# Top-k search of a sparse-attention layer: two groups of three blocks in place of four groups

## The chip, the cores and the metric

One core of one Trainium2 chip runs the whole layer in one launch. The metric is the device time of one execution in microseconds (us), as the median of several runs. Engines are named TensorE (PE; PEld is its weight load), VectorE (DVE), ScalarE (ACT), GpSimd (POOL) and SyncE (SP, which issues loads).

## What is computed

A hybrid decoder layer over 1024 tokens of width 1024, batch 1: a token mixer of two attention groups, a cross attention to 256 memory tokens, and a convolutional GLU. The part that matters here is group A, attention over the 256 best keys by a separate index score, per query and causal:

```python
logits = jnp.einsum('bqhd,bsd->bqhs', qib, k_idx)
score = jnp.einsum('bqh,bqhs->bqs', wib, jax.nn.relu(logits)).astype(jnp.float32)
score = jnp.where(causal[None], score, -jnp.inf)
_, idx = lax.top_k(score, topk)
...
s = jnp.where(valid[:, :, None, :], s, -jnp.inf)
p = jax.nn.softmax(s, axis=-1).astype(v.dtype)
return jnp.einsum('bqhk,bqkd->bqhd', p, v_sel)
```

Group B is differential attention over all causal keys: (softmax(q1 k1) - lam softmax(q2 k2)) v, with 4 heads.

## The kernel before, in words

The 1024 queries are eight blocks of 128; block i sees (i + 1) * 128 keys. Blocks 0 and 1 have at most 256 keys and need no search. For blocks 2 to 7 the kernel finds the 256th largest score of each row, turns it into an additive mask `mb[i]`, and computes group A densely with that mask.

The program runs in stages. **C**: the input projection in five column chunks (`proj_mm`, 24 matmuls a tile, evacuated by ScalarE at L618), with the index scores `sc[i]` made on the way (`idx_head`, L489 to L496). **B**: 32 units of group B, head by head and block by block in the order 7, 1, 6, 0, 5, 3, 4, 2 (`b_s`: scores, their evacuation with row minimum on VectorE at L746, the exponential on ScalarE at L748; `b_comb`: L756 to L758 on VectorE; `b_t`: transposes, copied by ScalarE at L654; `b_av`), mixed with the key and value projections of the memory (`mem_step`). **A**: 64 units of group A, block by block (`a_s`: scores, evacuated with the mask on VectorE at L991, the exponential at L992; then transposes and `a_av`), with the output projection behind it. Then cross attention and the GLU.

The search is a binary search on the bits of the threshold, 32 rounds from bit 31 to bit 0 (`topk_iter`). One round of a group handles all its blocks:

- On ScalarE ("act"): for each block a Sign of score minus candidate that adds up along the row (L525). VectorE then decides for each block whether the bit stays (L527), and makes the next candidate for the whole group (L529). The next round's Signs wait for it.
- On VectorE ("dve"): for each block a comparison that counts (L537), then two short instructions for the group, which have as many columns as it has blocks: L539 and L540 for the upper 16 bits, L542 and L543 for the lower 16. The upper half compares a 16-bit copy of the scores. After bit 16 the scores are narrowed into another 16-bit copy (L552 and L553, a pair for each 512 columns).

After bit 0 an end step for each block (`topk_mask`, L566 to L579) makes the mask: a count, two comparisons, a scan (L577) that settles ties in order of the keys, and two more passes.

The rounds wait in two queues, `topk_q["act"]` and `topk_q["dve"]`, group after group. A group's rounds may start when its last block's scores are there. `tick(us)` is called after each projection tile, each unit of B and A and each memory unit with the time that this piece is meant to take; where a queue's owed time reaches its `PACE` of the stage (C, B, A), the next round is issued at that place. `topk_finish(i)`, ahead of block i's scores in A, issues whatever of its group is left. The final order on each engine is set by the framework's scheduler, and each engine works through its list in order.

Of the kernel before, what the change touches and what calls it, by code (L numbers as in the profile page):

```python
# [44 lines left out]
def hybrid_layer(ctx, tc, I, out):  # L45
    nc = tc.nc
    pe, act, dve, pool, sp = nc.tensor, nc.scalar, nc.vector, nc.gpsimd, nc.sync
# [20 lines left out]
    def mtile(shape, dt, name):  # L68
        return along.tile(shape, dt, name=name)
# [429 lines left out]

    GROUPS = [(x.split("-")[0], tuple(int(y) for y in x.split("-")[1])) for x in 'act-23,act-6,dve-45,dve-7'.split(",")]
    cand = [mtile([P, 3], I32, f"cand{g}") for g in range(len(GROUPS))]
    ccnt = [mtile([P, 3], F32, f"ccnt{g}") for g in range(len(GROUPS))]
    crej = [mtile([P, 3], I32, f"crej{g}") for g in range(len(GROUPS))]
    cx = [mtile([P, 3], F32, f"cx{g}") for g in range(len(GROUPS))]
    U16 = mybir.dt.uint16
# [5 lines left out]
    def topk_iter(g, b):  # L513

        on, blocks = GROUPS[g]
        ng = len(blocks)
# [42 lines left out]
    def topk_mask(g, j):  # L559

        on, blocks = GROUPS[g]
        i = blocks[j]
# [24 lines left out]
    last = {}  # L587
    scored = [1]

    PACE = [dict(zip(("act", "dve"), [float(y) for y in x.split(",")])) for x in '4,6:4.5,10:4.5,5'.split(':')]  # L590
    phase = [0]

    def tick(us):

        pace = PACE[phase[0]]
        for on in ("act", "dve"):
# [1084 lines left out]
```

## Time and profile before

| | |
|---|---|
| median of 3 runs | 1703.17 us (1700.48 to 1704.67) |
| profiled execution | 1704.6 us, its span 1702.5 us |
| mean granted TensorE clock | 0.968 |
| TensorE busy | 1580.2 us, 93% of the span |
| VectorE busy | 1224.4 us, 72% |
| ScalarE busy | 788.5 us, 46% |
| GpSimd busy | 639.6 us, 38% |

The busy shares are averages over stages with different limits, so the rows further down are cut by stage: busy time of each engine in a stretch, what an engine waited for and who released it, and the mean duration of each kind of instruction. In the names, a number behind a buffer is left out; "jk<-mb,cx 128x768" writes jk and reads mb and cx, 128 partitions by 768 columns.

### The profile page before, as it was taken

What the parts mean: (1) busy time and instruction counts of PE and PEld (TensorE: products, weight loads), DVE (VectorE), ACT (ScalarE), POOL (GpSimd) and SP (SyncE); (2) the same over time, 40 slices, a digit from 0 to 9 for tenths busy, and PEclk for the clock granted to TensorE, in tenths of its full rate; (3) what the DMA queues carried; (4) which work ended last, traced back from release to release, by engine and by line L of the source; (5) the groups of instructions that cost most, each with busy time, mean ns of one, the idle gap of its engine ahead of it and who ended that gap; (6) DMA issues with size and microseconds to landing.
All of it is one profiled execution on the core that took longest, in us unless ns stands there. A gap on an engine that the chain in (4) does not pass through costs nothing.

```text
span 1702.5 us, 22404 instructions
## 1 busy us (share of the span) xinstructions
PE 1580.2 (93%) x7660; PEld 1294.8 (76%) x7660; DVE 1224.4 (72%) x2501; ACT 788.5 (46%) x1633; POOL 639.6 (38%) x787
## 2 busy tenths in 40 slices
PE   8899988778889999999999979999999999988889
PEld 7788766666678888878777857888888888876767
DVE  5746998998988674367552699766666667689974
ACT  6544677587777446325441235333333333433242
POOL 2646666534573352230010145222232221339831
PEclk9999999888989999999999989999999999998999
DMA  8321124212221222261211211222222225842221
GB/s 284 92 82 61 66 93 164 70 49 86 82 81 63 69 74 74 75 211 50 75 43 69 75 74 62 75 88 95 77 74 75 74 77 179 325 147 94 80 75 50
DMA packets 91745, 162.37 MB, mean 95 GB/s; under 512 B 14960, under 2 KB 34928, under 8 KB 91632
## 3 DMA queue, kind: packets, MB, share of 16 engines
q1 hardware_dynamic: 84736, 136.83, 24.7%
q10 hardware_dynamic: 5616, 19.93, 3.0%
q0 software_dynamic: 1280, 4.20, 0.6%
q8 instruction: 60, 0.98, 0.2%
q14 instruction: 53, 0.43, 0.1%
HBM read 126.32 MB, written 34.60 MB: 95 GB/s over the span
## 4 chain that ended last, share of the span: by engine, by line
PE 57%; DVE 27%; issue 7%; DMA 4%; ACT 3%; POOL 2%; SPq 0%; ACTq 0%; DVEq 0%; POOLq 0%
PE acc L281 9%; PE acc L282 9%; PE acc L283 9%; DVE wp L1547 5%; PE big L281 4%; PE big L282 4%; PE big L283 4%; PE trp L281 3%; DVE jk L537 3%; PE trp L282 3%; PE trp L283 3%; PE acc L1009 2%; DVE e L746 2%; PE big L1242 2%; DVE e L758 1%
## 5 line engine op out<-in xcount | busy, mean ns | idle before, releaser
L175 ACT CAST wp<-raw 128x512 fp32r<-128x512 f32 (+1 forms) x204 | 121.2, 615 | 228.5 <-POOL raw L201 127.8
L178 DVE TENSOR_TENSOR wp<-raw,wp 128x512 fp32r<-128x512 f32 (+1 forms) x168 | 134.9, 808 | 117.1 <-ACT wp L175 109.4
L178 POOL TENSOR_TENSOR wp<-raw,wp 128x512 fp32r<-128x512 f32 x84 | 113.5, 1369 | 47.3 <-ACT wp L175 46.5
L199 POOL TENSOR_TENSOR ws<-raw 128x512 f32<-128x512 f32 x21 | 28.4, 1353 | 271.9 <-DMA raw<-in_w_ffn_in_dram 216.4
L281 PE MATMUL acc<-wp,xh 128*128 128x512 f32 (+1 forms) x272 | 110.3, 407 | 9.6 <-ACT X L618 9.6
L282 PE MATMUL acc<-wp,xh 128*128 128x512 f32 (+1 forms) x272 | 110.1, 406 | 0.0
L283 PE MATMUL acc<-wp,xl 128*128 128x512 f32 (+1 forms) x272 | 109.9, 405 | 0.0
L177 POOL TENSOR_SCALAR wp<-raw 128x512 fp32r<-128x512 f32 (+1 forms) x48 | 33.7, 706 | 163.7 <-DVE rst L110 63.5
L654 ACT COPY pt<-trp 128x512 f32<-128x512 f32 (+3 forms) x144 | 66.1, 476 | 61.4 <-PE trp L663 61.1
L525 ACT ACTIVATE mb<-sc,cand 128x384 bf16<-128x384 f32 (+1 forms) x96 | 75.5, 787 | 38.6 <-DVE cand L529 34.5
L1009 PEld LDWEIGHTS acc<-va_t,pt 128*128 128x128 f32 x576 | 74.9, 195 | 9.8 <-ACT pt L654 7.9
L1009 PE MATMUL acc<-va_t,pt 128*128 128x65 f32 x576 | 77.0, 273 | 4.6 <-ACT pt L654 4.5
L991 DVE CUSTOM_DVE_ANT_0 ea<-big,mb,ra 128x384 f32<-128x384 f32 (+5 forms) x48 | 45.5, 948 | 36.9 <-PE trp L663 30.6
L281 PEld LDWEIGHTS acc<-wp,xh 128*128 128x128 f32 x272 | 52.9, 195 | 23.3 <-ACT X L618 11.8
L282 PE MATMUL acc<-wp,wp 128*128 128x512 f32 x152 | 62.3, 410 | 6.5 <-DVE wp L1547 3.8
L282 PE MATMUL big<-wp,wp 128*128 128x512 f32 x132 | 55.0, 416 | 12.4 <-DVE wp L1547 12.3
L281 PE MATMUL acc<-wp,wp 128*128 128x512 f32 x152 | 61.9, 407 | 3.8 <-ACT wp L1546 2.8
L992 ACT ACTIVATE ea<-ea,sta 128x128 f32<-128x128 f32 (+7 forms) x64 | 49.5, 777 | 27.5 <-DVE sta L991 26.4
L1547 DVE TENSOR_TENSOR wp<-ta,wp 128x512 fp32r<-128x512 f32 x55 | 50.7, 962 | 15.5 <-ACT wp L1546 15.5
L283 PEld LDWEIGHTS acc<-wp,xl 128*128 128x128 f32 x272 | 52.8, 194 | 11.5
L282 PEld LDWEIGHTS acc<-wp,xh 128*128 128x128 f32 x272 | 52.6, 194 | 11.3 <-issue 0.2
L283 PE MATMUL acc<-wp,wp 128*128 128x512 f32 x152 | 60.5, 398 | 0.0
(431 smaller groups left out, 5220.2 us busy)
## 6 DMA issues: line engine op xcount, KB each, us to landing
raw<-in_w_ffn_in_dram SPq DMA_DIRECT2D x44, 512.0 KB, 3.7
u_d<-fg ACTq DMA_DIRECT2D x22, 512.0 KB, 3.2
raw<-u_d SPq DMA_DIRECT2D x33, 256.0 KB, 3.1
raw<-in_w_in_dram SPq DMA_DIRECT2D x16, 512.0 KB, 3.9
raw<-in_w_out_dram SPq DMA_DIRECT2D x16, 512.0 KB, 3.6
xraw<-in_x_dram SPq DMA_DIRECT2D x8, 512.0 KB, 7.5
qk_d<-X SPq DMA_DIRECT2D x16, 256.0 KB, 2.0
raw<-in_w_xk_dram SPq DMA_DIRECT2D x8, 512.0 KB, 3.8
```

The source lines that it names most:

```text
L175: act.copy(pg[:, 0, :n], src)
L178: (dve if el == "d" else pool).tensor_tensor(pg[:, 1, :n], src, pg[:, 0, :n].bitcast(F32), op=OP.subtract)
L281: pe.matmul(o, lhsT=lh, rhs=rh, start=start, stop=False)
L282: pe.matmul(o, lhsT=lh, rhs=rl, start=False, stop=False)
L283: pe.matmul(o, lhsT=ll, rhs=rh, start=False, stop=stop)
L525: act.activation(mb[i], sc[i], AF.Sign, bias=cf[:, j:j + 1], scale=-1.0, accum_out=cnt[:, j:j + 1])
L537: dve.tensor_scalar(jk[:, :n], src, th[:, j:j + 1], None, op0=OP.is_ge, op1=OP.add, accum_out=cnt[:, j:j + 1])
L654: act.copy(dst, src)
L991: last["dve"] = dve.tensor_tensor_reduce(e[:, :n], S[:, :n], mask, ra[:, i, h:h + 1], 3.0e38, OP.add, OP.min, st[:, 0, h:h + 1])
L992: last["act"] = act.activation(e[:, :n], e[:, :n], AF.Exp, bias=st[:, 0, h:h + 1], scale=-1.0)
L1009: pe.matmul(acc[:, hh * 65:hh * 65 + 65], lhsT=pt, rhs=va_t[:, kt, :], start=kt == 0, stop=kt == i)
L1547: dve.tensor_tensor(pg[:, 1, :], v, pg[:, 0, :].bitcast(F32), op=OP.subtract)
```

## The change

Two lines. The four groups, (2, 3) and then (6) on ScalarE, (4, 5) and then (7) on VectorE, become two, (2, 3, 6) and (4, 5, 7). The pace, the time between rounds on each engine in C, B and A, is set anew.

```diff
@@ -499,7 +499,7 @@
-    GROUPS = [(x.split("-")[0], tuple(int(y) for y in x.split("-")[1])) for x in 'act-23,act-6,dve-45,dve-7'.split(",")]
+    GROUPS = [(x.split("-")[0], tuple(int(y) for y in x.split("-")[1])) for x in 'act-236,dve-457'.split(",")]
@@ -587,7 +587,7 @@
-    PACE = [dict(zip(("act", "dve"), [float(y) for y in x.split(",")])) for x in '4,6:4.5,10:4.5,5'.split(':')]
+    PACE = [dict(zip(("act", "dve"), [float(y) for y in x.split(",")])) for x in '5.5,8:8,10:4,5'.split(':')]
```

Group (2, 3, 6) can start when block 6's scores are there and group (4, 5, 7) when block 7's are; the first had to wait for block 3, the second for block 5.

How instructions stand on an engine before and after shows at three places. First ScalarE in C, from one projection tile's squares (L629, t2) to the next tile's evacuation (L618, X); mb is the Signs' output by block. Before:

```order
L629 ACTIVATE t2_285_2013<-X_282_1999 128x512
L525 ACTIVATE mb2_930,ccnt0_523<-sc2_931,cand0_519 128x384
L525 ACTIVATE mb3_932,ccnt0_523<-sc3_933,cand0_519 128x512
L525 ACTIVATE mb2_930,ccnt0_523<-sc2_931,cand0_519 128x384
L525 ACTIVATE mb3_932,ccnt0_523<-sc3_933,cand0_519 128x512
L618 ACTIVATE X_288_2051<-acc_287_2026,rx_72 128x512
```

and with the change:

```order
L629 ACTIVATE t2_277_1944<-X_273_1926 128x512
L525 ACTIVATE mb2_922,ccnt0_521<-sc2_923,cand0_519 128x384
L525 ACTIVATE mb3_924,ccnt0_521<-sc3_925,cand0_519 128x512
L525 ACTIVATE mb6_930,ccnt0_521<-sc6_931,cand0_519 128x896
L618 ACTIVATE X_280_1982<-acc_279_1957,rx_72 128x512
```

Two rounds of two Signs ahead of the evacuation have become one round of three; another such round stands ahead of the squares.

Second VectorE at the end of B, ahead of the first score evacuation of A (L991). Before, the last round of block 6 (two more such rounds stand between it and the last unit's L758) and the first instructions of its end step:

```order
L527 TENSOR_SCALAR crej1_528<-ccnt1_524 128x1
L529 SCALAR_TENSOR_TENSOR cand1_520<-crej1_528,cand1_520 128x1
L566 TENSOR_SCALAR mb6_938<-sc6_939,cand1_520 128x896
L569 ISA jk_896_4785,tks_535<-mb6_938,sc6_939 128x896
L569 ISA tks_535 128x1
L571 TENSOR_SCALAR jk_897_4787,ccnt1_524<-sc6_939,tks_535 128x896
L574 TENSOR_SCALAR mb6_938<-sc6_939,tks_535 128x896
L991 ISA ea_928_4926,sta_926_4922<-big_927_4923,tri_68,ra_75 128x128
```

and with the change, ahead of that L991, a round of blocks 4, 5 and 7 and the first count of the next (one more round stands between these rows and the last unit's L758):

```order
L537 TENSOR_SCALAR jk_933_4829,ccnt1_522<-mb4_926,cx1_526 128x640
L537 TENSOR_SCALAR jk_934_4831,ccnt1_522<-mb5_928,cx1_526 128x768
L537 TENSOR_SCALAR jk_935_4833,ccnt1_522<-mb7_932,cx1_526 128x1024
L542 TENSOR_SCALAR crej1_524<-ccnt1_522 128x3
L543 SCALAR_TENSOR_TENSOR cx1_526<-cx1_526,crej1_524 128x3
L537 TENSOR_SCALAR jk_942_4879,ccnt1_522<-mb4_926,cx1_526 128x640
L991 ISA ea_954_4920,sta_952_4916<-big_953_4917,tri_68,ra_75 128x128
```

Three short rounds and the start of an end step became seven counts and two decisions; what is left of the last round and the end steps of blocks 4, 5 and 7 stand behind this L991.

Third VectorE in A, at the first units of block 2. Before, a round of block 7 among the evacuations:

```order
L991 ISA ea_1048_5328,sta_1046_5324<-big_1047_5325,mb2_930,ra_75 128x384
L991 ISA sta_1046_5324 128x1
L537 TENSOR_SCALAR jk_1049_5333,ccnt3_526<-mb7_940,cand3_522 128x1024
L991 ISA ea_1053_5345,sta_1046_5324<-big_1052_5342,mb2_930,ra_75 128x384
L991 ISA sta_1046_5324 128x1
L539 TENSOR_SCALAR crej3_530<-ccnt3_526 128x1
L991 ISA ea_1057_5361,sta_1046_5324<-big_1056_5358,mb2_930,ra_75 128x384
L991 ISA sta_1046_5324 128x1
L540 SCALAR_TENSOR_TENSOR cand3_522<-crej3_530,cand3_522 128x1
```

and with the change, where the end step of block 7 is just finishing (L578 and L579):

```order
L991 ISA ea_1079_5342,sta_1073_5325<-big_1078_5339,mb2_922,ra_75 128x384
L991 ISA sta_1073_5325 128x1
L578 SCALAR_TENSOR_TENSOR jk_1011_5123<-sc7_933,tks_527,jk_1011_5123 128x1024
L991 ISA ea_1083_5358,sta_1073_5325<-big_1082_5355,mb2_922,ra_75 128x384
L991 ISA sta_1073_5325 128x1
L579 TENSOR_TENSOR mb7_932<-mb7_932,jk_1011_5123 128x1024
L991 ISA ea_1094_5388,sta_1073_5325<-big_1093_5385,mb2_922,ra_75 128x384
L991 ISA sta_1073_5325 128x1
```

Behind it the evacuations stand without any search between them.

## Rows read from the trace of the kernel before

**Rows 1.** Stretches C, B, A01, A2-7: length; busy PE, PEld, DVE, ACT, POOL; clock; DMA; GB/s

```profile
143.67:291.60 147.93, 131.55 (x543) 102.11 (x542) 133.99 (x350) 96.90 (x222) 97.34 (x156) 0.95 0.31 101
291.60:481.70 190.10, 152.79 (x888) 130.25 (x888) 173.71 (x475) 142.45 (x343) 88.79 (x143) 0.90 0.23 71
481.70:510.50 28.80, 23.49 (x133) 20.19 (x132) 26.27 (x77) 17.86 (x48) 22.62 (x37) 0.82 0.32 101
510.50:683.00 172.50, 165.78 (x1143) 147.78 (x1142) 113.73 (x249) 94.62 (x166) 62.93 (x113) 0.99 0.21 70
```

**Rows 2.** Waits of VectorE in B: engine, line, released by; us in total, times, longest

```profile
DVE crej L527 <- ACT mb L525: 5.9, 5, 1.7
DVE st L756 <- ACT e L748: 5.1, 5, 1.6
```

**Rows 3.** Waits of TensorE in C

```profile
PE acc L281 <- ACT X L618: 9.6, 5, 3.9
```

**Rows 4.** Waits of ScalarE in C

```profile
ACT mb L525 <- DVE cand L529: 26.5, 19, 3.2
```

**Rows 5.** Counts of VectorE, groups by line and form: busy us, mean ns

```profile
L537 DVE TENSOR_SCALAR_CACHE_REDUCE jk<-mb,cx 128x1024 bf16<-128x1024 uint16 x16 | 20.4, 1275 | 0.1
L537 DVE TENSOR_SCALAR_CACHE_REDUCE jk<-mb,cx 128x768 bf16<-128x768 uint16 x16 | 16.1, 1005 | 0.1
L537 DVE TENSOR_SCALAR_CACHE_REDUCE jk<-mb,cx 128x640 bf16<-128x640 uint16 x16 | 13.9, 871 | 0.0
L537 DVE TENSOR_SCALAR_CACHE_REDUCE jk<-sc,cand 128x1024 bf16<-128x1024 f32 x1 | 1.3, 1270 | 0.0
```

**Rows 6.** Decisions of VectorE, groups by line and form

```profile
L527 DVE TENSOR_SCALAR crej<-ccnt 128x1 int32<-128x1 f32 x96 | 13.1, 145 | 7.8 <-ACT mb L525 7.7
L529 DVE SCALAR_TENSOR_TENSOR cand<-crej,cand 128x1 int32<-128x1 int32 x32 | 8.1, 255 | 0.3
L542 DVE TENSOR_SCALAR crej<-ccnt 128x2 f32<-128x2 f32 x16 | 4.9, 305 | 0.0
L543 DVE SCALAR_TENSOR_TENSOR cx<-cx,crej 128x2 f32<-128x2 f32 x16 | 6.5, 404 | 0.1
L539 DVE TENSOR_SCALAR crej<-ccnt 128x2 int32<-128x2 f32 x16 | 4.7, 291 | 0.0
L540 DVE SCALAR_TENSOR_TENSOR cand<-crej,cand 128x2 int32<-128x2 int32 x16 | 7.8, 490 | 0.1
L542 DVE TENSOR_SCALAR crej<-ccnt 128x1 f32<-128x1 f32 x16 | 2.4, 151 | 0.4
L543 DVE SCALAR_TENSOR_TENSOR cx<-cx,crej 128x1 f32<-128x1 f32 x16 | 5.5, 345 | 0.4
```

**Rows 7.** Narrowing and end steps, groups by line over the span

```profile
L552 DVE TENSOR_SCALAR tk<-sc,cand,crej 128x512 f32<-128x512 f32 (+2 forms) x6 | 2.7, 489 | 0.1
L553 DVE TENSOR_TENSOR mb<-tk,cand 128x512 uint16<-128x512 uint16 (+2 forms) x6 | 3.3, 582 | 0.0
L571 DVE TENSOR_SCALAR_CACHE_REDUCE jk<-sc,cand 128x640 bf16<-128x640 f32 (+2 forms) x3 | 3.2, 1051 | 0.0
L574 DVE TENSOR_SCALAR mb<-sc,cand 128x640 bf16<-128x640 f32 (+2 forms) x3 | 3.0, 1016 | 0.0
L576 DVE TENSOR_SCALAR jk<-sc,cand 128x640 bf16<-128x640 f32 (+2 forms) x3 | 2.5, 842 | 0.0
L577 DVE TENSOR_TENSOR_SCAN sc<-jk 128x384 f32<-128x384 bf16 (+5 forms) x6 | 10.6, 1772 | 0.0
L578 DVE SCALAR_TENSOR_TENSOR jk<-sc,tks,jk 128x384 bf16<-128x384 f32 (+5 forms) x6 | 7.6, 1258 | 0.0
L579 DVE TENSOR_TENSOR mb<-mb,jk 128x384 bf16<-128x384 bf16 (+5 forms) x6 | 3.5, 577 | 0.1
```

**Rows 8.** Signs of ScalarE: the page's group, then block 6's form

```profile
L525 ACT ACTIVATE mb<-sc,cand 128x384 bf16<-128x384 f32 (+1 forms) x96 | 75.5, 787 | 38.6 <-DVE cand L529 34.5
L525 ACT ACTIVATE mb<-sc,cand 128x896 bf16<-128x896 f32 x32 | 33.3, 1041 | 11.3 <-DVE cand L529 8.0 <-DVE st L756 3.3
```

## Prediction

> **What bounds the kernel now.** First the stretches around the search: the rows of busy time per engine over four of them [rows 1]. I cut at fixed VectorE instructions, so that the same cuts can be found in the changed order: C, from the first head sum L631 to the first combination L758; B, from there to the first score evacuation L991 of group A; the first 16 L991 (blocks 0 and 1, "A01"); and the other 48 ("A2-7"). In C VectorE is busy 134.0 of 147.9 us and TensorE 131.6. In B VectorE is busy 173.7 of 190.1 us (91%), TensorE 152.8 at a granted clock of 0.90, ScalarE 142.5. In A01 VectorE has 26.3 of 28.8 us. In A2-7 this turns round: TensorE has 165.8 of 172.5 us, VectorE only 113.7. So a microsecond of VectorE work costs about its length in B and A01 and nearly nothing in A2-7. That is the row the rest hangs on.
>
> Then the waits. Of VectorE's 16.4 idle us in B it waited 5.9 for ScalarE's Sign counts (L527) and 5.1 for exponentials (L756) [rows 2]. In C TensorE waited 9.6 us for the projection evacuation L618 [rows 3], and ScalarE, whose queue L618 stands in, waited 26.5 us for a new candidate from L529 [rows 4]. Those two belong together: a Sign that waits for its candidate keeps the evacuation behind it waiting.
>
> **What the change does, in instructions.** The order of both programs gives the counts. VectorE's search instructions, before -> after:
> - C: counts L537 of 640 columns 20 -> 14, of 768 20 -> 14, of 1024 0 -> 14; L527 62 -> 66, L529 31 -> 22; decisions L539 with L540 16 -> 14 pairs, L542 with L543 4 -> 0; the narrowing L552 with L553 4 pairs -> 0.
> - B: counts 12 -> 18, 12 -> 17, 2 -> 17; L527 34 -> 30, L529 33 -> 10; L539/L540 2 -> 2, L542/L543 12 -> 15; narrowing 0 -> 6 pairs; the end steps (L571 to L579) of blocks 4 and 5 leave, the last four instructions of block 6's come in.
> - A01: 7 rounds of block 7 and the rest of block 6's end step go; the end steps of 4 and 5, one decision, two counts and two thirds of block 7's end step come.
> - A2-7: 23 counts of 1024 columns, 23 decisions, 2 narrowing pairs and an end step go; the last two instructions of block 7's end step are left.
>
> So the search, which before went on behind TensorE deep into A, is over before block 2 of A: what A2-7 had free moves forward into B.
>
> **The price of each.** A count takes 1275, 1005 and 871 ns by its columns [rows 5]; L527 145, L529 255 ns [rows 6]. The three-column decisions are in no row. The nearest are those of two columns, 305 + 404 ns (L542, L543) and 291 + 490 ns (L539, L540); I take these. Below, three columns might cost no more than one does, 151 + 345 ns; above, the third adds as much again as the second did. Either end is 0.2 us a round from what I take, 4 us over B's 17 rounds. A narrowing pair is 489 + 582 ns and one end step 1.05 + 1.02 + 0.84 + 1.77 + 1.26 + 0.58 = 6.5 us by the means of its lines [rows 7].
>
> B: counts 15 x 1.275 + 6 x 0.871 + 5 x 1.005 = +29.4; L527 -0.6; L529 -23 x 0.255 = -5.9; decisions 3 x 0.709 and wider L539/L540 = +2.8; narrowing 6 x 1.07 = +6.4; end steps -13.0 and +4.4. Sum **+23.5 us of VectorE work in B**. If all 16.4 idle us took it up, B would grow by 7; if its share of 91% stayed, by 26. I take a middle: of the 5.9 us behind L527 two thirds go, since 10 rounds of Signs stay in B out of 32 and more, and a third of the rest is filled by counts that wait for nobody: -7.5. **B +16.**
>
> A01: away 7 x (1.275 + 0.5) = 12.4 and 4.4 of block 6's end step; in come 2.3 for two counts, 0.7 for a decision, 13.0 and 4.7 of end steps, 20.7, so +3.9; VectorE's 2.5 idle us there hide little. **A01 +4.** It could be nothing if the three end steps fell into those gaps, and 6 if the long scan L577 of block 7 has L991 behind it.
>
> A2-7: 23 x 1.275 + 23 x 0.5 + 2 x 1.07 + 6.5 - 1.8 for what is left = 48 us of VectorE work vanish, but TensorE lacks only 6.7 us of being always busy. All of it is the most to be had, nothing the least; I take the middle. **A2-7 -3.**
>
> C: counts -6 x 0.871 - 6 x 1.005 + 14 x 1.275 = +6.6; L527 +0.6, L529 -2.3, L539/L540 -1.6, L542/L543 -2.8, narrowing -4.3: about -4 of VectorE. ScalarE gets longer rounds: all 96 Signs take 75.5 us, so three blocks' round is 2.36 us, and without block 6's Sign of 1041 ns it was 1.32 [rows 8]; 22 rounds of the one for 31 of the other are 52 us for 41; it is busy 96.9 of 147.9 us, so this has room. One round per projection tile stands between two evacuations where there were often two, so the round trip through VectorE is waited for once. Between nothing and all 9.6 us of TensorE's wait for L618: **C -4.**
>
> Order on the other queues: POOL's arithmetic and the loads of SP keep their places relative to the tiles; nothing is added there. POOL waits for VectorE's results as TensorE does, and has over half of B free [rows 1]. The pace numbers themselves issue nothing; they only set how many rounds stand between which tiles, and this is in the counts.
>
> **Sum.** 16 + 4 - 3 - 4 = +13 us on the profiled execution's 1704.6 us. That execution stands 1.4 us above the median 1703.2, so the forecast is **1716 us**. By the ends of the terms: least 7 - 4 + 0 - 6.7 - 9.6 = -13, most 26 + 4 + 6 = +36. The likeliest case by itself spans +6 to +23, 1709 to 1726.
>
> **The rivals.**
> *Nothing is absorbed.* VectorE's queue is in order; a round of three counts is 3.2 us in one piece where it was 1.9, and L746 and L758 of the next unit stand behind it. Then B keeps its 91% and grows by 26, A01 by 6, the wider decisions add some, and A gives nothing back: +30 to +36, 1733 to 1739. For it: no engine is nearer to always busy in B. Against: the counts can run in the gaps of rows 2.
>
> *The round trip was the cost (faster).* Place: C, where Signs stand ahead of L618. If the double round trips cause all of TensorE's stalls there, C gives back 9.6 us and A2-7 6.7; if at the same time ScalarE, rid of 22 rounds in B, lets VectorE's gaps be filled whole, B costs 7 and A01 2: -7, 1696. It decides if B's VectorE can come close to 100%; 91% over 190 us speaks against, ScalarE's 26.5 us for L529 [rows 4] for it.
>
> *Fewer instructions win everywhere (faster).* The search's VectorE work falls by 48 + 4 - 23.5 - 4 = 25 us in all. If VectorE set the end in every stretch, A2-7 too, the time would be 1678. Rows 1 speak against: A2-7 is TensorE's. The Trainium skill, VectorE: DVE Perf Modes, section Rules for kernel authors, says to minimize the number of VectorE operations, and by that rule this would be the expected way.
>
> *It comes to nothing.* B's gaps take up 12 of the 23.5 us, C and A repay the rest (12 of their 16): within 5 us of 1703. It needs three middling outcomes to come out well at once.
>
> The same section of the Trainium skill promises four times the rate for dense 16-bit scalar operations from SBUF to SBUF. Here the rows differ: the count of 1024 columns takes 1275 ns on 16-bit data and 1270 ns on the 32-bit scores of its first round [rows 5], so the sum has no such factor; at a quarter of the row, an estimate, B would get some 1.5 us instead of +23.5.
>
> **How the numbers follow.** Forecast 0.55; nothing absorbed 0.16; it comes to nothing 0.15; round trip 0.11; fewer instructions 0.03. A measurement of this kernel can tell about 0.3% (5 us) from no change, so slower is the first two, 0.71, the same 0.15, faster 0.14. For the range, 1701 to 1730: it leaves out the fastest cases (about 0.1) and the upper half of the unabsorbed one.
>
> **What would show it.** Right: B's stretch, first L758 to first L991, grows from 190 to about 206 us with VectorE busy near 197; A01 grows by about 4; A2-7 has VectorE under 70 us busy and TensorE above 97%; in C the wait for L618 is about halved. Wrong: B stays near 190 (then VectorE did not bound it), B grows beyond 215 (nothing absorbed), or A2-7 shrinks by more than its 6.7 idle us (then VectorE had bounded it in a way that busy shares hide).

## The result and the profile after

The changed kernel takes **1723.1 us** (median of 4 runs, 1721.7 to 1724.5) beside 1703.1 us for the kernel before: a ratio of 1.0112, 95% interval 1.0100 to 1.0125, so 1.1% slower. The forecast was 1716 us in 1701 to 1730. Two executions that took more than twice as long as the others, 5380.7 us (the profiled one of the first experiment) and 3925.0 us (one of the fourth), are left out of all that follows, so the first experiment has no stages. The profiled execution after took 1722.6 us with a span of 1720.6 us, against 1702.5 us before: 18.1 us to explain.

The same four stretches as in [rows 1], with the same columns. C is cut there at the fifth L631, not at the first one (which starts at 116.8 us before and 116.4 after); B and what follows do not depend on it:

```profile
143.22:292.82 149.60, 132.37 (x545) 103.21 (x544) 131.27 (x327) 107.16 (x229) 96.06 (x154) 0.94 0.31 98
292.82:504.59 211.77, 153.85 (x887) 131.21 (x885) 196.01 (x503) 132.68 (x336) 92.86 (x146) 0.88 0.21 67
504.59:536.64 32.05, 25.71 (x133) 21.98 (x133) 31.91 (x75) 18.99 (x48) 26.94 (x37) 0.77 0.30 99
536.64:701.93 165.29, 162.91 (x1140) 146.61 (x1139) 68.00 (x142) 93.88 (x163) 61.79 (x112) 1.00 0.21 68
```

More than the whole loss is in B: it grows from 190.1 to 211.8 us (+21.7), and VectorE's busy time in it from 173.7 to 196.0 (+22.3). A01 grows by 3.2, A2-7 shrinks by 7.2, B starts 1.2 us later (292.8 against 291.6), and what follows A is 0.8 shorter: 21.7 + 3.2 - 7.2 + 1.2 - 0.8 = 18.1.

What VectorE waited for in B after, as in [rows 2]:

```profile
DVE kb L698 <- ACT kb L697: 5.2, 1, 5.2
DVE e L746 <- PE big L739: 4.1, 5, 1.7
DVE st L756 <- ACT e L748: 2.2, 4, 0.9
DVE crej L527 <- ACT mb L525: 1.5, 3, 0.7
```

and the two rows of the kernel before, same view, which answer to the first two:

```profile
DVE e L746 <- PE big L739: 2.8, 3, 1.8
DVE kb L698 <- ACT kb L697: 0.4, 1, 0.4
```

The two waits of [rows 2] fell from 5.9 + 5.1 to 1.5 + 2.2 us, by 7.3. But L698 and L746 rose from 3.2 to 9.3, and VectorE's idle time in B is 15.8 us where it was 16.4. The waits changed their names, not their sum.

The new one is a single stall at a change of head. VectorE's timeline after (start us, us, instruction, idle before it); L698 finishes the next head's K once TensorE has transposed it (L695) and ScalarE has copied it (L697):

```profile
340.58 0.68 DVE L698 TENSOR_TENSOR kb<-trp,kb 128x512 fp32r<-128x512 f32 x1
341.18 0.16 DVE L542 TENSOR_SCALAR crej<-ccnt 128x3 f32<-128x3 f32 x1
341.25 0.61 DVE L758 SCALAR_TENSOR_TENSOR e<-e,st 128x384 f32<-128x384 f32 x1
341.77 0.15 DVE L543 SCALAR_TENSOR_TENSOR cx<-cx,crej 128x3 f32<-128x3 f32 x1
347.14 0.69 DVE L698 TENSOR_TENSOR kb<-trp,kb 128x512 fp32r<-128x512 f32 x1 [5.22 <-ACT kb L697]
```

TensorE's timeline after has 24 matmuls of the memory projection (L281 to L283) in these microseconds, ahead of the transposes that the stall waits for; the first, the last and the transposes:

```profile
338.62 0.77 PE L281 MATMUL acc<-wp,wp 128*128 128x512 f32 x1
...
345.52 0.39 PE L283 MATMUL acc<-wp,wp 128*128 128x512 f32 x1
345.75 0.60 PE L695 MATMUL trp<-ident,kdup 128*128 128x128 f32 x4
```

In the kernel before, VectorE's timeline at the same place, between the same two L698:

```profile
328.98 0.66 DVE L698 TENSOR_TENSOR kb<-trp,kb 128x512 fp32r<-128x512 f32 x1
...
335.30 1.01 DVE L537 TENSOR_SCALAR_CACHE_REDUCE jk<-mb,cx 128x768 bf16<-128x768 uint16 x1
...
336.76 0.88 DVE L537 TENSOR_SCALAR_CACHE_REDUCE jk<-mb,cx 128x640 bf16<-128x640 uint16 x1
...
337.68 1.01 DVE L537 TENSOR_SCALAR_CACHE_REDUCE jk<-mb,cx 128x768 bf16<-128x768 uint16 x1
...
338.62 0.69 DVE L698 TENSOR_TENSOR kb<-trp,kb 128x512 fp32r<-128x512 f32 x1
```

and the copy of ScalarE that L698 needs, in ScalarE's timelines before and then after:

```profile
337.05 0.59 ACT L697 CAST kb<-trp 128x512 fp32r<-128x512 f32 x1
```

```profile
346.53 0.58 ACT L697 CAST kb<-trp 128x512 fp32r<-128x512 f32 x1
```

Before, three rounds of counts (5.6 us of counting) stood in VectorE's queue beside the same matmuls. They made L698 start 1.0 us after its copy had ended (338.62 against 337.64); after, it starts at once, but VectorE has stood idle. So a round of search in B has no fixed price: beside such matmuls most of it was free, elsewhere it delays. The stall is VectorE time left unused, not time added at this place: from L698 to L698 it is 9.6 us before and 6.6 after.

### The profile page after: what moved, and what is told of

It is laid out like the page before. It is cut to its first block, busy times and chain, and to the rows that moved or that the text cites. A ratio compares the mean times of both kernels' runs of the same rounds, so it can differ in the third digit from the quotient of the medians.

```text
span 1720.6 us, 22313 instructions
## 1 busy us (share of the span) xinstructions
PE 1580.7 (92%) x7660; PEld 1295.9 (75%) x7660; DVE 1205.6 (70%) x2399; ACT 790.1 (46%) x1633; POOL 644.7 (37%) x787
## 3 DMA queue, kind: packets, MB, share of 16 engines
q1 hardware_dynamic: 84736, 136.83, 24.5%
## 4 chain that ended last, share of the span: by engine, by line
PE 57%; DVE 24%; issue 7%; DMA 6%; POOL 3%; ACT 3%; SPq 0%; ACTq 0%; DVEq 0%; POOLq 0%
PE acc L282 9%; PE acc L281 9%; PE acc L283 9%; DVE wp L1547 5%; DVE jk L537 4%; PE big L282 4%; PE big L283 4%; PE big L281 4%; PE trp L282 3%; PE trp L281 3%; PE trp L283 3%; DVE e L746 2%; PE acc L1009 2%; PE big L1242 2%; DVE e L758 1%
## 5 line engine op out<-in xcount | busy, mean ns | idle before, releaser
L281 PE MATMUL acc<-wp,xh 128*128 128x512 f32 (+1 forms) x272 | 110.4, 409 | 11.4 <-ACT X L618 11.4
L283 PE MATMUL acc<-wp,xl 128*128 128x512 f32 (+1 forms) x272 | 110.0, 405 | 0.0
L525 ACT ACTIVATE mb<-sc,cand 128x384 bf16<-128x384 f32 (+2 forms) x96 | 75.0, 784 | 24.7 <-DVE cand L529 18.0
L991 DVE CUSTOM_DVE_ANT_0 ea<-big,mb,ra 128x384 f32<-128x384 f32 (+5 forms) x48 | 45.6, 950 | 56.8 <-PE trp L663 48.4
L281 PEld LDWEIGHTS acc<-wp,xh 128*128 128x128 f32 x272 | 52.9, 194 | 24.2 <-ACT X L618 12.7
L281 PE MATMUL acc<-wp,wp 128*128 128x512 f32 x152 | 62.3, 410 | 5.1 <-ACT wp L1546 3.1
L748 ACT ACTIVATE e<-e,st 128x1024 f32<-128x1024 f32 (+7 forms) x64 | 49.5, 775 | 34.6 <-DVE st L746 33.5
L283 PE MATMUL acc<-wp,wp 128*128 128x512 f32 x152 | 61.5, 405 | 0.0
L283 PEld LDWEIGHTS acc<-wp,xl 128*128 128x128 f32 x272 | 52.9, 194 | 11.4
```

Source lines behind the costliest of these rows:

```text
L281: pe.matmul(o, lhsT=lh, rhs=rh, start=start, stop=False)
L283: pe.matmul(o, lhsT=ll, rhs=rh, start=False, stop=stop)
L525: act.activation(mb[i], sc[i], AF.Sign, bias=cf[:, j:j + 1], scale=-1.0, accum_out=cnt[:, j:j + 1])
L748: last["act"] = act.activation(e[:, :n], e[:, :n], AF.Exp, bias=st[:, c:c + 1], scale=-1.0, accum_out=st[:, 4 + c:5 + c])
L991: last["dve"] = dve.tensor_tensor_reduce(e[:, :n], S[:, :n], mask, ra[:, i, h:h + 1], 3.0e38, OP.add, OP.min, st[:, 0, h:h + 1])
```

## The experiments

Seven theories were put to the runs as they came up. **1**: VectorE's search work that the merged group moves ahead of A2-7 is paid in full there. **2**: the longer rounds cost, by their trip between engines. **3**: the new pace costs. **4**: VectorE stands idle at the head changes behind the memory matmuls. **5**: the lower granted clock in B costs. **6**: search is also the cover of VectorE's waits. **7**: stage C hangs on ScalarE's Signs. The table gives every kernel's stages (us, of the profiled execution; first L758 as the start of B; idle is B less VectorE's busy time in it; behind A is from the last L991 to the end of the span) and the median time.

| kernel | B starts | B | VectorE in B | idle | A01 | A2-7 | behind A | time | ratio, 95% interval |
|---|---|---|---|---|---|---|---|---|---|
| before | 291.6 | 190.1 | 173.7 | 16.4 | 28.8 | 172.5 | 1019.5 | 1703.1 | 1 |
| after | 292.8 | 211.8 | 196.0 | 15.8 | 32.1 | 165.3 | 1018.7 | 1723.1 | 1.0112, 1.0100 to 1.0125 |
| 1 new groups, old pace | | | | | | | | 1719.2 | 1.0088, 1.0071 to 1.0104 |
| 2 old groups, new pace | 283.0 | 202.0 | 172.7 | 29.3 | 32.9 | 180.4 | 1015.5 | 1714.3 | 1.0067, 1.0049 to 1.0086 |
| 3 ScalarE's group alone | 291.3 | 203.9 | 177.6 | 26.3 | 25.7 | 174.1 | 1018.9 | 1716.1 | 1.0076, 1.0059 to 1.0092 |
| 4 VectorE's group alone | 291.9 | 214.1 | 195.7 | 18.4 | 32.2 | 167.3 | 1016.0 | 1721.9 | 1.0106, 1.0089 to 1.0122 |
| 5 after, short counts of block 7 | 292.0 | 202.2 | 187.0 | 15.2 | 35.4 | 165.7 | 1015.1 | 1713.0 | 1.0057, 1.0037 to 1.0076 |
| 6 the second, memory behind K | 281.1 | 202.3 | 176.6 | 25.7 | 33.1 | 181.0 | 1017.6 | 1719.9 | 1.0105, 1.0077 to 1.0133 |
| 7 before, memory behind K | 292.0 | 200.9 | 178.7 | 22.2 | 24.9 | 173.2 | 1017.7 | 1709.8 | 1.0037, 1.0023 to 1.0050 |
| 8 the third, 4.5 for ScalarE in B | 290.3 | 196.0 | 175.4 | 20.6 | 24.0 | 172.0 | 1016.7 | 1702.7 | 1.0004, 0.9991 to 1.0016 |
| 9 after, 4.5 for ScalarE in B | 293.8 | 210.1 | 199.8 | 10.3 | 33.1 | 166.3 | 1014.6 | 1718.5 | 1.0088, 1.0072 to 1.0103 |
| 10 the second, 4.5 for ScalarE in B | 282.4 | 206.2 | 178.9 | 27.2 | 31.5 | 175.3 | 1015.3 | 1711.3 | 1.0046, 1.0031 to 1.0062 |
| 11 the eighth, 13 for VectorE in B | 290.8 | 195.0 | 170.5 | 24.5 | 25.4 | 172.6 | 1014.2 | 1701.8 | 0.9995, 0.9985 to 1.0004 |
| 12 before, 5.5 for ScalarE in C | 286.1 | 206.0 | 177.2 | 28.8 | 35.3 | 175.2 | 1014.9 | 1719.4 | 1.0089, 1.0072 to 1.0106 |

Behind A no search is left in any of these kernels, and yet this stretch differs by up to 5.3 us (1014.2 to 1019.5). A difference of that size between two times need not come from the search; the stages say where it lies.

**1. New groups, old pace.**

```diff
-... '5.5,8:8,10:4,5' ...
+... '4,6:4.5,10:4.5,5' ...
```

> The two groups of three with the old pace (4,6 : 4.5,10 : 4.5,5), so that only the groups differ from the kernel before. By the order and the durations of the rows, VectorE's work against the kernel before is +29 us in C, +19 in B, -15 in A01, -51 in A2-7. Theory 1 (VectorE work moved into C and B is paid, work in A2-7 is free): about 1728 us, 1718 to 1738, worse than the change. Theory 2 (it is the longer rounds that cost, wherever they stand): the rounds are as long as in the change, so near 1723. Theory 3 (the new pace costs, not the groups): back to 1703 within 5.

Measured 1719.2 us. That is in theory 1's range, at its lower end, and 4 us under theory 2's number. The groups alone bring 16 of the 20 us; that the old pace heals it (theory 3) is refuted. What the new pace adds on top, 4 us, is hardly told apart: the two intervals just overlap.

**2. Old groups, new pace.**

```diff
-... 'act-236,dve-457' ...
+... 'act-23,act-6,dve-45,dve-7' ...
```

> The four old groups with the new pace (5.5,8 : 8,10 : 4,5). VectorE's work against the kernel before: -19 us in C, +1 in B, -2 in A01, +19 in A2-7. Theory 1: C gets shorter by up to the 16 us that TensorE lacks there, A2-7 pays little: about 1695, 1688 to 1702, faster than both. Theory 2: the rounds are the short ones, so 1703. Theory 3: about 1723.

Measured 1714.3 us, which none of the theories had. B starts 8.6 us earlier; ten counts and 18 Signs fewer stand in C. But then B has 202.0 us with no more VectorE work than before:

```profile
283.00:485.02 202.02, 154.35 (x887) 132.33 (x887) 172.74 (x473) 131.60 (x335) 90.43 (x146) 0.88 0.22 69
```

and what VectorE waited for there begins with:

```profile
DVE kb L698 <- ACT kb L697: 14.3, 2, 8.2
DVE st L756 <- ACT e L748: 6.9, 8, 1.4
```

So theory 1 is not all: VectorE's idle time in B rose from 16.4 to 29.3 us, 14.3 of it in two stalls of the kind shown above. A2-7 grew by 7.9 us for 20 us more of VectorE's work; 14 of ScalarE's Signs stand there now as well.

**3. ScalarE's group merged alone.**

```diff
-... 'act-236,dve-457' ... '5.5,8:8,10:4,5' ...
+... 'act-236,dve-45,dve-7' ... '5.5,6:8,10:4,5' ...
```

> Only ScalarE's two groups merged (2, 3, 6), VectorE's groups as before (4, 5 and 7), pace 5.5,6 : 8,10 : 4,5. VectorE's work against the kernel before: -1 us in C, +2 in B, -8 in A01, 0 in A2-7. Theory 1: 1697, 1692 to 1704. Theory 2 with ScalarE's longer rounds as the cost (evacuations L618 behind three Signs): 1710 or more, with TensorE's wait for L618 in C above 11 us.

ScalarE has the new pace here too, VectorE the old one. Measured 1716.1 us; theory 1 had 1697 and missed. Theory 2's number came (1710 or more), its sign did not: TensorE's wait for L618 in C is 9.8 us, not above 11. B again grows, with 177.6 us of VectorE work:

```profile
291.32:495.18 203.86, 158.31 (x888) 136.18 (x888) 177.55 (x458) 132.45 (x336) 92.95 (x143) 0.87 0.21 66
```

**4. VectorE's group merged alone.**

```diff
-... 'act-236,dve-457' ... '5.5,8:8,10:4,5' ...
+... 'act-23,act-6,dve-457' ... '4,8:4.5,10:4.5,5' ...
```

> Only VectorE's two groups merged (4, 5, 7), ScalarE's as before (2, 3 and 6), pace 4,8 : 4.5,10 : 4.5,5. VectorE's work against the kernel before: -1 us in C, +26 in B, +5 in A01, -41 in A2-7. Theory 1: the whole cost is here, 1724, 1718 to 1730. Theory 2 with ScalarE's rounds as the cost: near 1703.

Here VectorE has the new pace (8 for 6 in C), ScalarE the old one. Measured 1721.9 us, as theory 1 had it:

```profile
291.92:506.00 214.08, 155.44 (x890) 133.13 (x890) 195.72 (x523) 144.34 (x348) 90.41 (x139) 0.86 0.21 64
```

This group alone brings the whole loss: 22.0 us more VectorE work than before in B, and B 24.0 us longer.

**5. The changed kernel with shorter counts of block 7.** Each count of block 7 leaves out 640 of its 1024 columns, so block 7's mask is another one.

```diff
+            if i == 7:
+                n, src = 3 * P, src[:, :3 * P]
             dve.tensor_scalar(jk[:, :n], src, th[:, j:j + 1], None, op0=OP.is_ge, ...
```

> The kernel after the change, with each of block 7's 32 counts looking at 384 of its 1024 columns (so block 7's threshold is another one). By the rows, a count falls from 1.27 us to about 0.61 us, an estimate from the counts of 640, 768 and 1024 columns: 0.66 us each. The trace of the kernel after has 14 of them in stage C, 17 in stage B and 1 in A01. Theory 1, VectorE's work that was moved ahead of A2-7 is paid in full: C -9, B -11, A01 -0.7, the time 1702 us. Theory 4, half of what VectorE does is beside TensorE's lumps of memory matmuls and so free: about 1712 us. Theory 2, what the longer rounds cost is the trip from count to count and not the counting: 1720 us or more.

Measured 1713.0 us, 10 us less than the kernel after; theory 4's number for the whole, but not in its way, and 3.6 of the 10 us lie behind A. Where a microsecond of VectorE costs is plain by stage:

```profile
292.01:494.20 202.19, 153.53 (x880) 131.67 (x879) 186.99 (x507) 131.36 (x335) 90.93 (x143) 0.88 0.21 64
```

In B, 9.0 us less work made 9.6 us less time: paid in full, as theory 1 says. In C some 9 us of counting (14 x 0.66) came out and B started 0.8 us earlier: there VectorE's counts cost nearly nothing, against theory 1. A01 took 3.4 us more, which no theory had.

**6 and 7. The memory projection behind the K transposes**, in the second experiment's kernel and, as control, in the kernel before:

```diff
-        mem_step(MB)
         if ok(s + 1):
             b_comb(s + 1)
         if s >= 0 and h < 3 and 2 <= m <= 5:
             b_k(h + 1, (m - 2) // 2, 4 * (m % 2))
+        mem_step(MB)
```

> The old four groups with the new pace (second experiment, 1714 us), and in each step of stage B the quarter of memory projection is issued behind the next head's K transposes instead of ahead of them. Theory 4, in the second experiment stage B grew because VectorE stood idle for 14.3 us in two places, before the subtraction of L698, while TensorE ran memory matmuls that stood in its queue ahead of the K transposes, and the slower rounds left nothing in VectorE's queue there: the two stalls fall from 8.2 and 6.1 us to under 2 us each, B comes from 202 to 190 to 194 us, the time to 1702 to 1707 us. Theory 5, B is longer because TensorE's granted clock fell from 0.90 to 0.88, and where VectorE waits follows from that: B stays at 202 us and the time at 1714 us, with the idle time before another line. Theory 3, slower pace costs as such: 1714 us.

> The control for the sixth: the kernel before, with the quarter of memory projection behind the K transposes too. In the kernel before, the wait of L698 was 0.4 us in stage B, since search instructions stood in VectorE's queue at those places. Theory 4: nothing to win there, 1703 us, within 3 us. If the other order helps whatever the pace (the transposes are simply earlier), it is 5 to 10 us faster than the kernel before, and the sixth experiment then says nothing on the pace.

Measured 1719.9 and 1709.8 us. The waits of VectorE in B of the sixth:

```profile
DVE st L756 <- ACT e L748: 10.7, 10, 2.3
DVE kb L698 <- ACT kb L697: 6.7, 1, 6.7
DVE e L746 <- PE big L739: 5.2, 6, 1.5
```

The wait at L698 fell from 14.3 to 6.7 us, and B stayed at 202.3: other waits took its place, and the edit costs the kernel before 7 us as well. Theory 4's stalls are there, but moving the matmuls does not give their time back. That B stays and the idle time moves is what theory 5, the clock, had forecast for the sixth. The seventh speaks against it:

```profile
292.03:492.97 200.94, 152.60 (x888) 129.43 (x888) 178.74 (x480) 143.28 (x344) 92.68 (x139) 0.91 0.22 68
```

B is 200.9 us long at a granted clock of 0.91, and was 190.1 at 0.90. And in the kernel after, at 0.88, TensorE's busy time in B is only 1.1 us above the kernel before (153.9 against 152.8), so the clock does not make its 21.7 us. Whether it has a share in the others is not shown.

**8. The third experiment with ScalarE's old pace in B.**

```diff
-... '5.5,6:8,10:4,5' ...
+... '5.5,6:4.5,10:4.5,5' ...
```

The other number that changes, ScalarE's pace in A, acts on nothing: in both kernels all 96 Signs stand ahead of A.

> The third experiment (blocks 2, 3 and 6 in one group on ScalarE, VectorE's two groups left, 1716 us), with ScalarE's pace in stage B back at 4.5 us a round instead of 8. VectorE's instructions in each stage are the same sum, only the places where ScalarE's decisions stand in VectorE's queue move. Theory 3, the slow pace in B costs 12 us there: B from 204 to 190 to 194 us, the time 1702 to 1706 us. Theory 4, what matters is whether something stands in VectorE's queue ahead of the subtractions of L698 at the head changes; with the quick pace these rounds are used up in the first half of B and the later head changes stay empty: B 200 to 204 us, the time 1712 to 1717 us. Theory 2, the three-block round on ScalarE is what costs, as it holds ScalarE for its three sweeps at a time: 1716 us or more, with more waits of VectorE for ScalarE.

Measured 1702.7 us, 13 us less than the third and equal to the kernel before:

```profile
290.26:486.26 196.00, 154.41 (x886) 132.18 (x887) 175.43 (x458) 133.76 (x337) 96.66 (x146) 0.89 0.23 70
```

Theory 2 falls: the three-block round on ScalarE costs nothing here. Theory 4's number (1712 to 1717) falls too. Theory 3 holds for this kernel, though its range for B (190 to 194) was too low; the wait at L698 went from 7.6 to 1.7 us.

**9. The changed kernel with ScalarE's old pace in B.**

```diff
-... '5.5,8:8,10:4,5' ...
+... '5.5,8:4.5,10:4,5' ...
```

> The kernel after the change (two groups of three blocks), with only ScalarE's pace in stage B back from 8 to 4.5 us a round. With VectorE's two old groups the same edit gave 13 us (third against eighth experiment: 1716.1 and 1702.7), though VectorE's work in each stage stayed. Theory 3, the pace costs the same whatever the groups: 1723 - 13 = 1710 us, stage B 198 to 204 us. Theory 6, the slow pace costs only where VectorE stands idle for want of other work, and the group of blocks 4, 5 and 7 has filled stage B (196.0 us busy of 211.8): nothing to win, 1720 to 1725 us, stage B 209 to 214 us.

Measured 1718.5 us:

```profile
293.81:503.88 210.07, 152.97 (x888) 130.00 (x886) 199.80 (x507) 133.88 (x336) 93.57 (x146) 0.89 0.22 68
```

The edit that was worth 13 us in the third is worth 4 to 5 here, and by the profiled executions these do not come from the search: at the end of A2-7 this kernel is 1.3 us behind the kernel after (703.2 against 701.9 us), and behind A it is 4.1 us shorter. So theory 6, nothing to win, holds; its range for B has the 210.1. VectorE's idle time in B is down to 10.3 us, the lowest of all, and the time is still 15 us above the kernel before: with the merged group, the work itself is the length of B.

**10. The second experiment with ScalarE's old pace in B**, and here its old pace in A too:

```diff
-... '5.5,8:8,10:4,5' ...
+... '5.5,8:4.5,10:4.5,5' ...
```

> The second experiment (old four groups, new pace, 1714.3 us), with only ScalarE's pace in stage B back from 8 to 4.5 us a round. Theory 3, ScalarE's pace in B is what the new pace costs with the old groups: stage B from 202.0 to 190 to 194 us, C stays 9 us shorter than in the kernel before, the time 1702 to 1706 us. Theory 1, VectorE's work that the slower C leaves over is what costs (B +5 of work by the order, A2-7 +13): 1712 to 1717 us.

Measured 1711.3 us, under theory 1's range by 0.7 and far over theory 3's. B did not come back but grew, by 4.1 us for 6.2 us more VectorE work; A2-7, where the second still had 14 Signs and this kernel has none, is 5.1 us shorter:

```profile
282.42:488.58 206.16, 155.09 (x886) 133.50 (x884) 178.93 (x503) 146.49 (x364) 91.94 (x146) 0.88 0.22 67
```

A rule "ScalarE's slow pace in B costs 13 us" is thus refuted: it held for one set of groups.

**11. The eighth with fewer VectorE rounds in B.**

```diff
-... '5.5,6:4.5,10:4.5,5' ...
+... '5.5,6:4.5,13:4.5,5' ...
```

> The eighth experiment (blocks 2, 3 and 6 in one group on ScalarE, 1702.7 us), with VectorE's pace in stage B at 13 us a round instead of 10. By the order and the rows' durations 6.6 us of search move out of B, nearly all to A2-7. Theory 1, VectorE's work costs its whole length in B and, by the kernel after (46 us less of it made A2-7 7.2 us shorter) and the second experiment (20 us more of it made A2-7 8 us longer), 0.16 to 0.4 of its length in A2-7: B -6.6, A2-7 +1.0 to +2.6, the time 1697 to 1699 us, a little below the kernel before. Theory 6, search is what covers VectorE's waits in B, so that taking it away leaves idle time: B shortens by less than half of 6.6 us, the time 1702 to 1706 us.

Measured 1701.8 us, no different from the kernel before. B lost 4.9 us of VectorE work and 1.0 us of time; the wait at L698 went from 1.7 to 5.3. That is theory 6's outcome, if 0.2 us faster than its range. Its stretch B, and VectorE's wait there:

```profile
290.79:485.75 194.96, 152.94 (x888) 131.95 (x888) 170.50 (x440) 132.18 (x335) 94.33 (x135) 0.89 0.22 70
```

```profile
DVE kb L698 <- ACT kb L697: 5.3, 2, 4.2
```

**12. The kernel before with one pace number changed.**

```diff
-... '4,6:4.5,10:4.5,5' ...
+... '5.5,6:4.5,10:4.5,5' ...
```

> The kernel before with one number changed: ScalarE's pace in stage C at 5.5 us a round instead of 4. The new pace with the old groups made stage C 8.6 and 9.2 us shorter (second and tenth experiments), with 18 sweeps fewer on ScalarE and 10 counts fewer on VectorE in it; taking 8 us of counting alone from VectorE in C made it 0.8 us shorter (fifth). Theory 7, ScalarE's sweeps in C are what its length hangs on, as TensorE waits for ScalarE's evacuations there: C 5 to 9 us shorter than in the kernel before, with about 16 sweeps fewer; B, with ScalarE's pace as before, 190 to 196 us, and the time 1696 to 1702 us. Theory 1, it is VectorE's work: by the order 4 us of it leave C, C 0 to 2 us shorter, B 2 us longer, the time 1703 to 1706 us.

Measured 1719.4 us: one number costs 15 us. Theory 7 is right on C (44 Signs in place of 62, B starts 5.5 us earlier) and neither theory on the rest:

```profile
286.08:492.06 205.98, 155.17 (x884) 131.77 (x882) 177.15 (x494) 149.69 (x371) 89.89 (x146) 0.88 0.22 67
```

B is 15.9 us longer for 3.5 us more VectorE work. The eighth has the same paces and differs from this kernel by ScalarE's merged group alone, and it takes 1702.7 us: at these paces that merge is worth 17 us, while the old groups with the old paces are as fast. Neither a group nor a pace has a price by itself.

**What the runs settle, and what not.** Where VectorE has 187 us of work or more in B (after; 4, 5, 9), B is that work and 10 to 18 us, and the fourth and fifth show work that is added or taken out paid in full. Where it has 170 to 179 us, B is anywhere from 190 to 206 us; the kernel before, at 190.1, is the lowest of the nine. There the length hangs on where the rounds stand between the units, and the idle time is spread over waits for the exponential, the scores, the Signs and the K transposes. Which single placement rule keeps B at 190 us is **open**: the one tried for the K transposes moved the wait and not the end. No version beats the kernel before by more than can be measured.

## Why the prediction was right, and where not

The direction, the place and the main term stood: the search leaves a stretch that TensorE sets for one that VectorE sets. Term by term:

- **VectorE's work in B**, "+23.5 us": +22.3. The counts of instructions behind it, by stretch, are those of the trace.
- **What is absorbed**, "-7.5", and with it **B +16**: the step that failed. "Of the 5.9 us behind L527 two thirds go", and more is filled by counts: those waits did shrink, by 7.3 us, nearly the number forecast. What was missed is that a wait filled in one place says nothing of the others: rounds that stood beside the memory matmuls before were now elsewhere, VectorE stood idle for 5.2 us ahead of L698, and the sum stayed (16.4, 15.8). So 0.6 us were absorbed and not 7.5. That nothing is absorbed was the first rival, and B's +21.7 is nearer to its +26 than to the forecast; A01 and A2-7 did not follow the rival, and the total lies nearer to the forecast than to its 1733.
- **A01 +4**: +3.2, and that is luck in part. VectorE's work grew by 5.6 us (26.3 to 31.9), not by 3.9, and the 2.5 idle us that were to "hide little" hid 2.4 of it: VectorE is busy 31.9 of 32.1 us.
- **A2-7 -3**, at most 6.7: -7.2, which the prediction had named as a sign of being wrong. VectorE's busy time fell to 68.0 (under 70, as forecast) and TensorE is busy 98.6%. Of the 7.2, idle time of TensorE gave 6.7 - 2.4 = 4.3, and 2.9 came from its busy time, 165.8 to 162.9, at a granted clock of 1.00 for 0.99. The bound took the busy time as fixed, which it was not. VectorE's work there was not "nearly nothing" either: between the ends of the table A2-7 rises by 0.23 us for one of VectorE's busy time in it (165.7 us at 66.5 in the fifth, 181.0 at 133.9 in the sixth), though not evenly (172.5 at 113.7 before, 175.2 at 114.2 in the twelfth).
- **C -4**: +1.2 at the start of B. Single traces of kernels with the same instructions in C differ there by up to 1.9 us (281.1 to 283.0 in 2, 6 and 10), so the +1.2 itself says little; the 4 us did not come. The wait for L618 was to be halved; TensorE's and ScalarE's waits in C after, as in [rows 3, 4]:

```profile
PE acc L281 <- ACT X L618: 11.4, 3, 6.6
ACT mb L525 <- DVE cand L529: 18.0, 14, 2.6
```

The round trips did fall (26.5 to 18.0 us on ScalarE), but 11.4 us of TensorE's wait are now in three pieces, the longest 6.6. ScalarE's busy time in C rose from 96.9 to 107.2 us, and "this has room" was the wrong half of the step: the twelfth and the eighth have the same 22 rounds in C, one with 44 Signs and one with 66, and start B at 286.1 and 290.3 us, so Signs in C do cost. The eighth, with the same 66 Signs in C as after, starts B 1.3 us before the kernel before, so trips saved and Signs added about cancel there.

The sum forecast was +13 and is +18 on the profiled execution: B short by 5.7 and C by 5.2, against 4.2 too little credit in A2-7 and 0.8 too much cost in A01, and 0.8 after A. That the time came within 7 us of the forecast is partly luck: about half of the misses in B and C was made up by those of the other way. The rival "round trip was the cost" is refuted in B by the ninth (idle down to 10.3 us, still 1718.5), "fewer instructions win" by the result itself: 102 VectorE instructions fewer, and 1.1% slower.

## What to carry to other kernels

Ask of work that is moved which stretch pays for it: VectorE's cost 1.0 us for one in a stretch that it filled, 0.16 (the kernel after) to 0.4 (the second experiment) in one that TensorE set, and nearly nothing in C (one experiment). A forecast that waits will be filled must go through all waits of the stretch, not the two largest, since work that fills one is missing at another. And a pace table that was searched for one order of work is a point, not a slope: a single number changed in it cost 15 us, where the whole change cost 20.

## What the runs showed of the hardware that was not expected

The decisions on three columns were bounded by 496 ns a pair from below; they took less than those on two. From the groups by line and form of the kernel after:

```profile
L542 DVE TENSOR_SCALAR crej<-ccnt 128x3 f32<-128x3 f32 x16 | 3.0, 189 | 0.1
L543 DVE SCALAR_TENSOR_TENSOR cx<-cx,crej 128x3 f32<-128x3 f32 x16 | 3.5, 218 | 0.1
```

against 305 and 404 ns in [rows 6]. The means of [rows 6] were no price by width. The view of one line (least, median, longest ns), of the kernel before and then after:

```profile
L543 DVE SCALAR_TENSOR_TENSOR cx<-cx,crej x32: 148/160/1528, 253.5 to 623.9; 128x2 f32<-128x2 f32 x16, 128x1 f32<-128x1 f32 x16
```

```profile
L543 DVE SCALAR_TENSOR_TENSOR cx<-cx,crej x16: 148/158/565, 336.3 to 509.5; 128x3 f32<-128x3 f32 x16
```

The median is 0.16 us in both; a few take up to ten times that before, and up to 3.6 times after. VectorE's and GpSimd's timelines of the kernel before show what the long ones have in common:

```profile
201.00 1.28 DVE L540 SCALAR_TENSOR_TENSOR cand<-crej,cand 128x2 int32<-128x2 int32 x1
```

```profile
200.97 1.29 POOL L641 TENSOR_TENSOR X<-X,t 128x512 f32<-128x512 f32 x1 [2.95 <-DVE crej L539]
```

GpSimd's instruction began 0.03 us earlier, and VectorE's 0.15 us of work ended with it. All the decisions over 0.3 us (49 before, 21 after) end with a GpSimd instruction in this way. Their time over 0.15 us adds to about 25 us before and 11 after, and that is most of the 18.8 us by which VectorE's busy time fell over the span (1224.4 to 1205.6 us): VectorE's busy time holds waiting. The Trainium skill, SBUF — State Buffer, section Who interferes with whom, has VectorE and GpSimd take turns at a shared port where VectorE reads two tensors from SBUF, and GpSimd reads there, or where VectorE runs in a two-port mode, and the later one blocks until the first is done; these rows agree. Of the 49, 12 are L539 and L542, which read one tensor; that they ran in such a mode no run shows. The same section of the Trainium skill leaves the form that writes out its accumulator out of those modes, and the counts, which are of that form, took 1271 ns for 1024 columns of 16 bits after and 1275 before [rows 5], and no count of either kernel took over 1281.
